# Splitting the norms around the last feed forward into two halves of 128 tokens

## The chip, the cores and the metric

The kernel runs on one core of a Trainium2 chip. The metric is the device time of one launch in microseconds (us), the median of several runs. In the profile PE is TensorE's matmul part and PEld its weight loads, DVE is VectorE, ACT is ScalarE, POOL is GpSimd and SP is SyncE, whose queue issues nearly all transfers.

## The reference

Two transformer blocks stand one behind the other, on 256 tokens of width 1024 in float32. What matters here is the end of the second block, whose last layer takes a neighbourhood attention and then a feed forward on the latent stream alone:

```python
h = gated_residual(h, ml, 1, yl, 1.0)              # yl = attention output @ w_o
h = gated_residual(h, ml, 2, swiglu(ada_in(h, norm_g[i, 2], ml, 2), ffn_w_in[i, 1], ffn_w_out[i, 1]), 0.5)
return rms_norm(h, final_norm_g)

def ada_in(h, g, m, j):
    xn = rms_norm(h, g)                            # over the 1024 features of each token
    return xn * (1.0 + m[:, j, 1][:, None]) + m[:, j, 0][:, None]

def swiglu(x, w_in, w_out):                        # hidden width 2816
    a, b = jnp.split(x @ w_in, 2, axis=-1)
    return (jax.nn.silu(a) * b) @ w_out
```

Both norms that are changed go over the features of a token, so tokens can be taken in any grouping.

## The kernel before

Activations lie feature-major: 8 tiles (KC) of 128 features by 256 tokens (T). `xs[LAT][k]` is the residual of the latent stream. A product adds matmuls into a PSUM tile `acc` (three buffers). Numbers are split in two fp32r parts, so one product step is three matmuls in `mm3` (L400 to L402: whi with hh, wlo with hh, whi with hl), and each matmul has a load of its own 128x128 weights. `load_w` fetches a block of weights (SP queue), and ScalarE (L391) and VectorE (L392) split it into `whi` and `wlo`, four buffers each.

The class `Sq` collects the sum of squares of the residual for the next norm. Its `parts` are slices of the tokens. `add` squares a tile (ScalarE) and adds it up (GpSimd, L484). `end` does the last two tiles of one part, `close` multiplies by a matrix of ones to sum over features (L507 and L508, plain float32, two matmul records each), and `rstd` follows with Ln and Exp on ScalarE (L455, L457).

`grow` makes the 8 output tiles of a product and closes each into the residual (L1053). With an `Sq` the last two tiles, k = 6 and 7, are made part by part: all parts of a PSUM tile share that tile, and as soon as a part of both is there, its norm is closed. `ada` makes the normalized tiles hh and hl from the residual, part by part: two VectorE operations (L1041, L1043) and one of ScalarE (L1042) for each tile. In `ffn` the first pair of products goes through `lead`, which walks over the same parts; all later products take all tokens at once. `ffn` has 22 such pairs (f), then `grow` with the down projection, whose contraction is in three pieces of 8, 7 and 7 tiles; only the last piece carries the `Sq`.

In the earlier feed forwards two streams of 256 tokens are the two parts (`STREAMS`). The attention `nat` of the last layer and the last feed forward have only the latent stream, and before the change one part of 256 tokens. After that the kernel scales the residual by rstd and the final gain into tiles `fin` (L1398 on VectorE for six, L1395 on GpSimd and L1396 on ScalarE for k = 1 and 4) and stores them in three transfers (L1399).

The order on each engine is fixed when the kernel is built: the tile framework orders the instructions of each engine by their readiness in its plan and adds the semaphores, so that an engine's queue may hold work of a later line ahead of work of an earlier one. On the chip each queue runs in that order.

Of the kernel before, what the change touches and what calls it, by code (L numbers as in the profile page):

```python
# [13 lines left out]
ALU = mybir.AluOpType  # L14
# [215 lines left out]
def body(tc, a, off, outs, stop=None):  # L230
# [4 lines left out]
    def tl(pl, shape, tag, dt=F32, bufs=None):  # L235
        uid[0] += 1
        kw = {} if bufs is None else {"bufs": bufs}
        return pl.tile(shape, dt, tag=tag, name=f"{tag}_{uid[0]}", **kw)
# [31 lines left out]
    def V(name, i=None):  # L270
        lo, hi = off["vec"][name]
        return vec[:, lo:hi] if i is None else vec[:, lo + i:lo + i + 1]
# [37 lines left out]
    def G(l, v, j, k):  # L310
        return mod[l][2][:, v, j * 8 + k:j * 8 + k + 1]
# [714 lines left out]
    LAT, CTX = 0, 1  # L1026
    both = (LAT, CTX)
    STREAMS = [slice(0, T), slice(T, 2 * T)]

    def ada(l, j, sq, vs):  # L1030

# [15 lines left out]
    def grow(l, j, vs, prod, sq=None):  # L1047

        N = T * len(vs)

        def close(k, p, i):
            d = xs[vs[i]][k]
            dve.scalar_tensor_tensor(d, p[:, i * T:i * T + T], G(l, vs[i], j, k), d, ALU.mult, ALU.add)  # L1053
            return d

        for k in range(KC - 2 if sq else KC):
            p = acc([P, N])
            prod(k)(p, slice(0, N))
            ds = [close(k, p, i) for i in range(len(vs))]
            if sq:  # L1060
                sq.add(*ds)
        if sq:
            tail = [(k, prod(k), acc([P, N])) for k in (KC - 2, KC - 1)]
            for i, c in enumerate(sq.parts):
                for k, f, p in tail:
                    f(p, c)
                sq.end(i, *[close(k, p, i) for k, f, p in tail])
                sq.close(i)

    def ffn(l, s, j, sq, vs, nparts, every=2):  # L1070

        N = T * len(vs)
        h = ada(l, j, sq, vs)
        nsq = Sq(nparts)
        pace(0)
        with mk(f"ffn{l}{s}") as fp:
            for n, (lo, hi) in enumerate(THIRDS):
                us = []
                if n == 0 and N == T:
                    tl(fp, [P, G2], "gap")  # L1080
                for f in range(lo, hi):
                    if f == 3:
                        pace(every)
                    w = [load_w(a["fin"][2 * l + s, 2 * f + i]) for i in range(2)]
                    if f == 0:
                        pa, pb = lead(w, h, sq.parts)
                    else:
                        pa, pb = acc([P, N]), acc([P, N])
                        mmw(pa, w[0], h)
                        mmw(pb, w[1], h)  # L1090
                    g = tl(fp, [P, N], "sig", bufs=2)
                    sigmoid(g, pa)
                    dve.tensor_tensor(g, pa, g, ALU.mult)
                    dve.tensor_tensor(g, pb, g, ALU.mult)  # L1094
                    u = [tl(fp, [P, N], n_, F32R, bufs=12) for n_ in ("uh", "ul")]
                    split(g, *u)
                    us.append(u)

                def prod(k):
                    w = load_w(a[f"fout{n}"][2 * l + s, k])  # L1100
                    if n == 2 and k == 2:
                        pace(0)
                    return lambda p, c: mmw(p[:, c], w, [cut(u, c) for u in us])
                grow(l, j, vs, prod, nsq if n == 2 else None)
        return nsq
# [157 lines left out]
    def nat(sq):  # L1263
        l, j = 1, 1
        en = ExitStack()
        np_ = en.enter_context(mk("nat"))
        h = ada(l, j, sq, both)
        hl = [cut(t, slice(0, T)) for t in h]
        qs_, ks_, os_ = {}, {}, {}
        vs_ = [tl(np_, [P, D], f"nv{t}") for t in range(4)]  # L1270

        def query(i, p):
            qs_[i] = tl(np_, [P, T], "nq", bufs=3)
            act.activation(qs_[i], p, AF.Copy, scale=0.125)

        def key(i, p):
            ks_[i] = tl(np_, [P, 2 * T], "nk", bufs=3)
            act.activation(ks_[i], p, AF.Copy)

        def project(i):  # L1280
            if i not in qs_:
                query(i, dense(a["nqkv"][i], hl))
            key(i, dense(a["nqkv"][8 + i], h))

        def values(b):
            w = [load_w(a["nv"][b, i]) for i in range(2)]
            for t in range(4):
                p = acc([P, T])
                token_major(w, h, t, p)
                act.activation(vs_[t][:, b * T:b * T + T], p, AF.Copy)  # L1290

        O = {}

        def unit(h2, qt):

            es_ = []
            Ss = [att([P, 2 * T]) for _ in range(2)]
            for hh in range(2):
                rows = slice(64 * hh, 64 * hh + 64)
                pe.matmul(Ss[hh], qs_[h2][rows, qt * P:qt * P + P], ks_[h2][rows, :], start=True, stop=True)  # L1300
            for hh in range(2):
                S = Ss[hh]
                bias = tl(np_, [P, T], "nb", bufs=4)
                nc.sync.dma_start(bias, a["nbias"][2 * h2 + hh, :, qt * T:qt * T + T])
                dve.tensor_tensor(S[:, :T], S[:, :T], bias, ALU.add)
                mx = tl(mini, [P, 1], "mx1")
                dve.tensor_reduce(mx, S, axis=AX.X, op=ALU.max)
                dve.tensor_scalar(mx, mx, -1.0, None, op0=ALU.mult)
                e = tl(np_, [P, 2 * T], "ne", bufs=4)
                sm = tl(mini, [P, 1], "sm1")  # L1310
                act.activation(e, S, AF.Exp, bias=mx, accum_out=sm)
                dve.reciprocal(sm, sm)
                dve.tensor_scalar(e, e, sm, None, op0=ALU.mult)
                es_.append(e)
            yield
            pts = []
            for e in es_:
                tp = nrm([P, 4, P])
                for kt in range(4):
                    pe.transpose(tp[:, kt], e[:, kt * P:kt * P + P], ident)  # L1320
                PT = tl(np_, [P, 4, P], "npt", bufs=4)
                act.activation(PT, tp, AF.Copy)
                pts.append(PT)
            yield
            if qt == 0:
                O[h2] = acc([P, T])
            for kt in range(4):
                for hh in range(2):
                    c = 64 * (2 * h2 + hh)
                    pe.matmul(O[h2][64 * hh:64 * hh + 64, qt * P:qt * P + P], vs_[kt][:, c:c + 64], pts[hh][:, kt],  # L1330
                              start=kt == 0, stop=kt == 3)
            if qt == 1:
                if h2 == 0:
                    tl(np_, [P, G3], "gap")
                os_[h2] = [tl(np_, [P, T], f"{n}{h2}", F32R) for n in ("noh", "nol")]
                split(O[h2], *os_[h2])

        for i, p in enumerate(lead([load_w(a["nqkv"][i]) for i in range(2)], hl, [slice(0, T)])):
            query(i, p)
        project(0)  # L1340
        pace(2)
        for m in range(4):
            put(values, m)
            put(project, 2 * m + 1)
            if m < 3:
                put(project, 2 * m + 2)
                put(lambda: None)
        weave([unit(h2, qt) for h2 in range(8) for qt in range(2)], 1)
        os_ = [os_[i] for i in range(8)]
        nsq = Sq([slice(0, T)])  # L1350

        def prod(k):
            w = load_w(a["nwo"][k])
            return lambda p, c: mmw(p[:, c], w, [cut(o, c) for o in os_])
        grow(l, j, (LAT,), prod, nsq)
        en.close()
        return nsq
# [26 lines left out]
    finish(1, 1)  # L1384
    sq = nat(sq)
    finish(1, 2)
    sq = ffn(1, 1, 2, sq, (LAT,), [slice(0, T)])
    r = sq.rstd(0)
    with mk("fin") as fp:
        for lo, hi in ((0, 3), (3, 6), (6, 8)):  # L1390
            t = tl(fp, [P, hi - lo, T], f"fin{lo}")
            for k in range(lo, hi):
                d = t[:, k - lo]
                if k in (1, 4):
                    pool.tensor_tensor(d, xs[LAT][k], r, ALU.mult)  # L1395
                    act.activation(d, d, AF.Copy, scale=V("fg", k))  # L1396
                else:
                    dve.scalar_tensor_tensor(d, xs[LAT][k], V("fg", k), r, ALU.mult, ALU.mult)  # L1398
            nc.sync.dma_start(outs[0][:, lo:hi], t)  # L1399
    es2.close()  # L1400
    es.close()

# [17 lines left out]
```

## Time and profile before

| what | value |
|---|---|
| median of 3 runs | 2899.43 us (2898.97 to 2900.85) |
| profiled execution | 2906.19 us, span 2904.4 us |
| mean granted TensorE clock | 0.996 |
| busy: PE, PEld, DVE, ACT, POOL | 2867.7, 2551.6, 1973.9, 1409.4, 240.3 us |
| chain that ended last, by engine | PE 91%, DVE 5%, ACT 2%, DMA 1%, issue 1% |

The span goes from the first to the last instruction of the profiled execution; times inside it are us from its start. Matmuls are pipelined and their ends are modelled, so the pace of a row of them is read from the distance of their starts and not from their durations. The granted clock is given as a share of 2.4 GHz; 0.50 is the lower level, 1.2 GHz.

### The profile page before, as it was taken

Reading aid. Unit: us, or ns where it says so; the run is one execution under the profiler, and the core shown is the slowest. Engines: PE = TensorE matmul, PEld = TensorE weight load, DVE = VectorE, ACT = ScalarE, POOL = GpSimd, SP = SyncE. Lnnn points to the kernel's source line nnn. Section 1 sums busy time; section 2 is a strip of 40 time slices with the busy share of each in tenths; the row PEclk is TensorE's granted clock in tenths of the full one; section 3 lists DMA queues with packets and bytes.
Section 4 is the critical chain, followed back from the end, with each engine's and each line's share of the span. In section 5 each row is a group of like instructions: output and inputs, shape, how many; then the busy total and the mean of one; then the engine's idle time right before and its main releaser. Section 6 shows DMA issues by size and latency. Waiting matters only on the chain.

```text
span 2904.4 us, 46127 instructions
## 1 busy us (share of the span) xinstructions
PE 2867.7 (99%) x18084; PEld 2551.6 (88%) x18084; DVE 1973.9 (68%) x3370; ACT 1409.4 (49%) x2487; POOL 240.3 (8%) x216
## 2 busy tenths in 40 slices
PE   8999999999999999999999999999999999999998
PEld 7899999989899988888888888888888888887998
DVE  8787876888887666655776757656566665555665
ACT  7767664677765432334433435332343323444554
POOL 2121100212201000001110101000010000100000
PEclk9999999999999999999999999999999999999999
DMA  6344666544467544443343333444434443333564
GB/s 206 118 125 137 195 202 206 172 132 153 152 211 233 187 149 142 144 148 96 120 142 120 109 116 97 148 146 146 131 116 146 143 146 124 109 93 97 166 183 139
DMA packets 122906, 424.46 MB, mean 146 GB/s; under 512 B 13632, under 2 KB 20160, under 8 KB 122560
## 3 DMA queue, kind: packets, MB, share of 16 engines
q1 hardware_dynamic: 121248, 419.50, 45.9%
q8 instruction: 143, 2.34, 0.3%
q10 hardware_dynamic: 1440, 2.00, 0.2%
q14 instruction: 75, 0.61, 0.1%
HBM read 420.40 MB, written 1.05 MB: 145 GB/s over the span
## 4 chain that ended last, share of the span: by engine, by line
PE 91%; DVE 5%; ACT 2%; DMA 1%; issue 1%; POOL 0%; DVEq 0%; SPq 0%; POOLq 0%; ACTq 0%
PE acc L400 28%; PE acc L402 28%; PE acc L401 28%; DVE wlo L392 1%; PE att L652 1%; ACT whi L391 1%; DMA raw<-in_wmod_dram 1%; PE att L850 1%; PE att L400 1%; PE att L401 1%; PE att L402 1%; PE acc L1330 0%; PE nr L1320 0%; PE att L1300 0%; DVE dump L327 0%
## 5 line engine op out<-in xcount | busy, mean ns | idle before, releaser
L400 PE MATMUL acc<-hh,whi 128*128 128x512 f32 (+2 forms) x3200 | 1052.8, 329 | 12.4 <-ACT hh L528 6.3
L391 ACT ACTIVATE whi<-raw 128x1024 fp32r<-128x1024 f32 (+2 forms) x650 | 678.7, 1045 | 787.9 <-PE acc L402 730.0
L401 PE MATMUL acc<-hh,wlo 128*128 128x512 f32 (+2 forms) x3200 | 1046.1, 327 | 2.8 <-DVE wlo L392 2.8
L402 PE MATMUL acc<-hl,whi 128*128 128x512 f32 (+2 forms) x3200 | 1043.4, 327 | 0.3 <-DVE hl L1043 0.3
L392 DVE TENSOR_TENSOR wlo<-raw,whi 128x1024 fp32r<-128x1024 f32 (+2 forms) x650 | 789.3, 1215 | 331.6 <-ACT whi L391 296.0
L400 PEld LDWEIGHTS acc<-hh,whi 128*128 128x128 f32 x3200 | 605.1, 189 | 74.8 <-ACT hh L528 6.2
L401 PEld LDWEIGHTS acc<-hh,wlo 128*128 128x128 f32 x3200 | 604.1, 189 | 54.8 <-DVE wlo L392 3.5
L402 PEld LDWEIGHTS acc<-hl,whi 128*128 128x128 f32 x3200 | 603.0, 189 | 53.2 <-DVE hl L1043 0.7
L327 DVE SCALAR_TENSOR_TENSOR dump<-raw,cs 128x1024 bf16<-128x1024 f32 x288 | 355.4, 1234 | 260.1 <-DMA raw<-in_wmod_dram 257.4
L400 PE MATMUL acc<-uh,whi 128*128 128x256 f32 (+2 forms) x1258 | 407.0, 324 | 0.0
L402 PE MATMUL acc<-ul,whi 128*128 128x256 f32 (+2 forms) x1258 | 406.2, 323 | 0.2
L401 PE MATMUL acc<-uh,wlo 128*128 128x256 f32 (+2 forms) x1258 | 406.0, 323 | 0.0
L402 PEld LDWEIGHTS acc<-ul,whi 128*128 128x128 f32 x1258 | 237.1, 188 | 19.9 <-DVE ul L450 0.8
L400 PEld LDWEIGHTS acc<-uh,whi 128*128 128x128 f32 x1258 | 236.6, 188 | 19.1
L401 PEld LDWEIGHTS acc<-uh,wlo 128*128 128x128 f32 x1258 | 236.6, 188 | 19.1
L484 POOL TENSOR_TENSOR sqacc<-sqacc,sq 128x256 f32<-128x256 f32 (+2 forms) x60 | 75.6, 1260 | 1854.0 <-ACT sq L479 1756.3
L1053 DVE SCALAR_TENSOR_TENSOR x<-acc,gmod,x 128x256 f32<-128x256 f32 x136 | 65.8, 483 | 154.1 <-PE acc L402 153.5
L461 ACT ACTIVATE sig<-acc 128x512 f32<-128x512 f32 (+1 forms) x88 | 48.0, 546 | 252.2 <-PE acc L402 252.2
L400 PE MATMUL acc<-whi,hh 128*128 128x256 f32 x384 | 109.5, 285 | 0.4 <-ACT pd L1155 0.2
L402 PE MATMUL acc<-wlo,hh 128*128 128x256 f32 x384 | 109.1, 284 | 0.0
L401 PE MATMUL acc<-whi,hl 128*128 128x256 f32 x384 | 108.9, 284 | 0.0
L1094 DVE TENSOR_TENSOR sig<-acc,sig 128x512 f32<-128x512 f32 (+1 forms) x88 | 55.0, 624 | 33.3 <-PE acc L402 27.7
(319 smaller groups left out, 3530.0 us busy)
## 6 DMA issues: line engine op xcount, KB each, us to landing
raw<-in_fin_dram SPq DMA_DIRECT2D x176, 512.0 KB, 3.7
raw<-in_wmod_dram SPq DMA_DIRECT2D x144, 512.0 KB, 4.1
raw<-in_wf_dram SPq DMA_DIRECT2D x128, 512.0 KB, 4.3
raw<-in_win_dram SPq DMA_DIRECT2D x104, 512.0 KB, 3.7
raw<-in_fout_dram SPq DMA_DIRECT2D x64, 448.0 KB, 3.4
raw<-in_fout_dram SPq DMA_DIRECT2D x32, 512.0 KB, 3.6
raw<-in_rin_dram SPq DMA_DIRECT2D x32, 512.0 KB, 3.6
raw<-in_wbr_dram SPq DMA_DIRECT2D x24, 512.0 KB, 3.6
```

The source lines that it names most:

```text
L327: dve.scalar_tensor_tensor(dump, raw, 1.0, cs[:, v], ALU.mult, ALU.mult, accum_out=m[:, v, b:b + 1])
L391: act.activation(hi[:, :n], raw[:, :n], AF.Copy)
L392: dve.tensor_tensor(lo[:, :n], raw[:, :n], hi[:, :n].bitcast(F32), ALU.subtract)
L400: pe.matmul(out, w[0], x[0], start=start, stop=False)
L401: pe.matmul(out, w[1], x[0], start=False, stop=False)
L402: pe.matmul(out, w[0], x[1], start=False, stop=stop)
L461: act.activation(dst, src, AF.Exp, scale=-1.0, **k)
L484: eng.tensor_tensor(self.acc[:, :N], self.acc[:, :N], s[:, :N], ALU.add)
L652: pe.matmul(S[:, c:c + n], q[rows, t0 - q0:t0 - q0 + P], k[rows, 0:n], start=False, stop=i == ns - 1)
L850: pe.matmul(Z[:m, c + lo - k0:c + n], sbk[h2][rows, k0:k0 + m], sbq[h2][rows, lo - q0:Q], start=False, stop=k0 == 0)
L1053: dve.scalar_tensor_tensor(d, p[:, i * T:i * T + T], G(l, vs[i], j, k), d, ALU.mult, ALU.add)
L1094: dve.tensor_tensor(g, pb, g, ALU.mult)
```

## The change

The attention's `Sq` and the last feed forward's `Sq` get two parts of 128 tokens in place of one of 256. Thereby the last two tiles of the attention's output product and of the last down projection, the `ada` of the last feed forward and the first pair of its products are made in two halves. `close` in `grow` takes a slice of tokens in place of a stream's number. The final scaling and the stores go half by half: each half has its own rstd, six VectorE operations, two of GpSimd with two of ScalarE, and three stores whose rows on a partition are two or three pieces of 128 numbers.

```diff
+    HALVES = [slice(0, P), slice(P, T)]
@@ grow
-        def close(k, p, i):
-            d = xs[vs[i]][k]
-            dve.scalar_tensor_tensor(d, p[:, i * T:i * T + T], G(l, vs[i], j, k), d, ALU.mult, ALU.add)
+        def close(k, p, c):
+            v = vs[c.start // T]
+            d = xs[v][k][:, c.start % T:c.start % T + c.stop - c.start]
+            dve.scalar_tensor_tensor(d, p[:, c], G(l, v, j, k), d, ALU.mult, ALU.add)
             return d
...
-            ds = [close(k, p, i) for i in range(len(vs))]
+            ds = [close(k, p, slice(i * T, i * T + T)) for i in range(len(vs))]
...
-                sq.end(i, *[close(k, p, i) for k, f, p in tail])
+                sq.end(i, *[close(k, p, c) for k, f, p in tail])
                 sq.close(i)
@@ nat
-        nsq = Sq([slice(0, T)])
+        nsq = Sq(HALVES)
@@ end of the kernel
-    sq = ffn(1, 1, 2, sq, (LAT,), [slice(0, T)])
-    r = sq.rstd(0)
+    sq = ffn(1, 1, 2, sq, (LAT,), HALVES)
     with mk("fin") as fp:
-        for lo, hi in ((0, 3), (3, 6), (6, 8)):
-            t = tl(fp, [P, hi - lo, T], f"fin{lo}")
...
+        for i, c in enumerate(HALVES):
+            r = sq.rstd(i)
+            for lo, hi in ((0, 3), (3, 6), (6, 8)):
+                t = tl(fp, [P, hi - lo, P], f"fin{i}{lo}")
+                for k in range(lo, hi):
+                    d = t[:, k - lo]
+                    if k in (1, 4):
+                        pool.tensor_tensor(d, xs[LAT][k][:, c], r, ALU.mult)
+                        act.activation(d, d, AF.Copy, scale=V("fg", k))
+                    else:
+                        dve.scalar_tensor_tensor(d, xs[LAT][k][:, c], V("fg", k), r, ALU.mult, ALU.mult)
+                nc.sync.dma_start(outs[0][:, lo:hi, c], t)
```

## Rows read from the trace of the kernel before

**Rows 1.** Busy time and share of each engine, on the page.
```profile
PE 2867.7 (99%) x18084; PEld 2551.6 (88%) x18084; DVE 1973.9 (68%) x3370; ACT 1409.4 (49%) x2487; POOL 240.3 (8%) x216
```

**Rows 2.** First and last matmul of both tail products, in time: start, duration, engine, what.
```profile
2694.57 0.28 PE L400 MATMUL acc<-noh,whi 128*128 128x256 f32 x1
...
2699.90 0.28 PE L402 MATMUL acc<-nol,whi 128*128 128x256 f32 x1
...
2889.15 0.28 PE L400 MATMUL acc<-uh,whi 128*128 128x256 f32 x1
...
2893.98 0.28 PE L402 MATMUL acc<-ul,whi 128*128 128x256 f32 x1
```

**Rows 3.** Stages behind the attention: length, busy PE, PEld, DVE, ACT, POOL, granted clock, DMA.
```profile
2700.00:2704.40 4.40, 1.57 (x6) 0.59 (x4) 2.94 (x6) 2.82 (x6) 0.00 (x0) 0.86 0.49 149
2704.40:2710.00 5.60, 5.60 (x26) 5.60 (x27) 5.42 (x14) 2.98 (x7) 0.00 (x0) 0.50 0.18 72
```

**Rows 4.** Chain that ended last, 2690 to 2720: start, us, what.
```profile
2701.62 0.71 PE nr L508 x2
...
2704.40 0.58 PE acc L400
```

**Rows 5.** The same chain at the kernel's end.
```profile
2894.30 0.50 DVE x L1053
...
2895.29 0.71 PE nr L508 x2
2896.03 0.48 ACT rln L455
...
2896.98 1.05 DVE fin L1398
2898.03 0.87 DVEq L1415
2898.90 1.58 DVE fin L1398 x4
```

**Rows 6.** Weight loads and matmuls of the stick-breaking attention, in order of time.
```profile
685.32 0.19 PEld L870 LDWEIGHTS nr<-t,nonesr 128*128 128x128 f32 x1
685.43 0.19 PEld L869 LDWEIGHTS nr<-t,nonesr 128*128 128x128 f32 x1
685.54 0.19 PEld L870 LDWEIGHTS nr<-t,nonesr 128*128 128x128 f32 x1
...
685.46 0.31 PE L869 MATMUL nr<-t,nonesr 128*128 128x144 f32 x1
...
685.61 0.22 PE L870 MATMUL nr<-t,nonesr 128*128 128x32 f32 x1
```

**Rows 7.** 128-column matmuls in time, and by shape (busy, mean ns).
```profile
2623.14 1.09 PE L1330 MATMUL acc<-npt,nv 128*64 128x128 f32 x16
...
2624.17 1.09 PE L1320 MATMUL nr<-ident,ne 128*128 128x128 f32 x8
...
L1330 PE MATMUL acc<-npt,nv 128*64 128x128 f32 x256 | 18.4, 279 | 0.0
```

**Rows 8.** One operation at two widths, by shape, on VectorE and on ScalarE.
```profile
L906 DVE SCALAR_TENSOR_TENSOR e<-e,rc,e 128x272 f32<-128x272 f32 x8 | 4.0, 495 | 0.0
...
L906 DVE SCALAR_TENSOR_TENSOR e<-e,rc,e 128x144 f32<-128x144 f32 x8 | 2.9, 362 | 0.0
...
L664 ACT ACTIVATE e<-att,mx,qs 128x272 f32<-128x272 f32 x32 | 18.5, 578 | 20.2 <-DVE mx L660 17.6 <-PE att L652 2.1 <-DVE rc L667 0.3
L664 ACT ACTIVATE e<-att,mx,qs 128x144 f32<-128x144 f32 x32 | 14.9, 466 | 0.0
```

**Rows 9.** End of the feed forward with two streams, in order of time.
```profile
2496.41 0.70 PE L508 MATMUL nr<-sqp,ones 128*128 128x256 f32 x2
...
2501.26 0.28 PE L400 MATMUL acc<-hh,whi 128*128 128x256 f32 x1
```

**Rows 10.** Transfers of the result: count, KB each, us to landing.
```profile
out_dram<-fin SPq DMA_DIRECT2D x2, 384.0 KB, 2.7
```

More of the change, by code (lines that the diff above doesn't have):

```diff
@@ L1386, in body @@
     finish(1, 2)
-    sq = ffn(1, 1, 2, sq, (LAT,), [slice(0, T)])
-    r = sq.rstd(0)
+    sq = ffn(1, 1, 2, sq, (LAT,), HALVES)
     with mk("fin") as fp:
-        for lo, hi in ((0, 3), (3, 6), (6, 8)):
-            t = tl(fp, [P, hi - lo, T], f"fin{lo}")
[L1392 to L1399, printed above, removed]
+        for i, c in enumerate(HALVES):
[10 more added lines that the diff above has]
+                nc.sync.dma_start(outs[0][:, lo:hi, c], t)
     es2.close()
```

## The prediction

> **What bounds the kernel now.** I read the page first: TensorE is busy for 99% of the span [rows 1], so a cut pays only where TensorE stands still or runs slowly, and every matmul that is added costs its full price. Then I looked for those places around the two norms that the change touches, in three views. In the order of time, the last two products before each norm (k = 6 and 7) are 48 matmuls that start every 0.1134 us in front of the last feed forward (2694.57 to 2699.90, 47 steps) and 42 that start every 0.1178 us behind it (2889.15 to 2893.98, 41 steps) [rows 2]. In the table by stages, the 4.4 us after the first of these blocks hold six matmuls at a falling clock, and the 5.6 us after that hold 26 matmuls at a granted clock of 0.50, the lower level (1.2 GHz), 0.215 us each [rows 3]. In the chain of waits the path through that hole is norm work: the ones-matmul at 2701.62, then Ln, Exp, the first normalized tile, and TensorE resumes at 2704.40 [rows 4]. At the end of the kernel the same chain is bare: close, square, ones-matmul, Ln, Exp, then 3.50 us of scaling, then the stores, with no matmul beside any of it [rows 5]. So there are two holes: one of 4.39 us (2700.01, one step after the start of the last product, to 2704.40) with a clock loss behind it, and one of 10.3 us (2894.10 to 2904.4).
>
> **What the change adds.** Three blocks of 256-column matmuls become twice as many of 128 columns: the 48 of the attention output product (k = 6, 7), the 48 of the first pair of feed-forward products (`lead` walks over the parts of the norm), and the 42 of the last down projection (k = 6, 7). In `mm3` each matmul loads its own 128x128 weights, so the number of loads doubles too: 276 pairs in place of 138. The whole question is the price of one such pair. Before has no run of 128-column fp32r matmuls, so I bound it.
> The lower end is by columns: half of 0.1134, that is 0.057 us; 128-column matmuls with 64-column weights do start every 0.054 us (1.09 less one duration of 0.28, over 15 steps) [rows 7]. The upper end is by loads. In the stick-breaking attention, fp32r matmuls of 144 and 32 columns alternate, each with its own 128x128 load; their columns need about 0.04 us each on average (88 x 0.1134 / 256), yet the loads start every 0.11 us [rows 6]. Transposes of exactly 128 columns with 128-column weights start every 0.116 us (1.09 less 0.28, over 7 steps), twice as far apart as those with half the weights [rows 7]. So the load sets the pace whenever the columns take less than that, and 256 columns are about the point where both are equal. I take 0.11, the fp32r row, with 0.105 to 0.117 as its own margin, and keep 0.057 for the range.
> 276 x 0.11 = 30.4 us in place of 96 x 0.1134 + 42 x 0.1178 = 15.8: **+14.5**.
> Three of the four closings now have their two ones-matmuls inside the stream of products, where before they stood in a hole: a 256-column ones-matmul is two records, so 4 records x 0.11 = 0.44 each: **+1.3**.
>
> **What it takes away.** In front, the norm of half 0 can run while half 1's products run. Chain: half 0 ends at 2694.57 + 5.3 = 2699.9; close to Exp took 2.88 us at the end of the kernel (2894.10 to 2896.98) [rows 5], about 2.4 with half the columns (below), then one scale and one activation of some 0.4 each: first tile at about 2703.1. Half 1 with its pair of ones-matmuls keeps TensorE until 2705.6. The cover is thus some 2.5 us longer than the chain, and VectorE's two operations per tile at about 0.3 us each (half 0: 16 of them, 4.8 us) stay ahead of TensorE's six matmuls per tile (0.66 us). The same structure exists in the kernel with two streams of 256 tokens, and there the ones-matmul stands among the second stream's products (2496.41) and the next stage's first matmul follows at 2501.26 without a hole [rows 9]. So I take the whole hole as gone, **-4.4**, and the stretch at the lower clock with it: 5.60 us for 26 matmuls against 26 x 0.1134 = 2.95, **-2.65**. What is late next is half 1's norm; it has the 5.3 us of half 0's `lead` matmuls to hide behind. If that cover were gone, up to 2.4 us would come back. The weight buffers of k = 6 and 7 are held some 5.6 us longer than now, but the next weights (f = 1) are not needed before `lead` ends. `lead`'s second accumulator waits for the close of k = 6 of half 1, and that product ends 24 matmuls ahead of `lead`: no wait.
> At the end, half 0's norm, scaling and stores lie beside half 1's products; only half 1's are bare, at 128 columns. What 128 columns are worth: the same scalar_tensor_tensor took 495 ns at 272 and 362 at 144, the same activation 578 and 466 [rows 8], so 0.13 us on VectorE and 0.11 on ScalarE. One close, three activations and a shorter drain of the ones-matmul: 0.13 + 0.34 + 0.05 = 0.5. Six scalings: 0.8 of the 3.50. **-1.3**. GpSimd's and ScalarE's two tiles ride beside them as now. The stores are six in place of three, in pieces of 512 B rather than 2 or 3 KB. Their landing took 2.7 us for 384 KB [rows 10], and I leave the last one at that; half 0's have left the queue by then. If small pieces are slower, up to 1.5 us is added; if the halved traffic helps, 0.3 is saved. Half 0's six scalings (about 2 us) may stand ahead of half 1's close on VectorE: 0 to 0.8 us. The other squares and sums cost the same in two pieces, beside matmuls.
>
> **Sum.** +14.5 + 1.3 - 4.4 - 2.65 - 1.3 = **+7.5 us**. The profiled execution took 2906.2 us with a span of 2904.4, so it lies 6.8 us above the median of the runs, 2899.43; I add the difference to the median: **2906.9 us**. About 0.2% (5.8 us) is what a measurement of this kernel can tell from no change, so this is slower by little more than that.
>
> **A rule beside the rows.** The loads in rows 6 stand 0.11 us apart, and that alone sets my price. The Trainium skill, "TensorE: Matmul & The Clock Gate", section "Back-to-back issue gap", says that a stream of load and matmul pairs at 128 columns settles at about 81 ns each. By that figure the price would be an estimated 276 x 0.081 = 22.4 in place of 30.4, and the sum -0.5 us. Rows 6 and 7 disagree with it for these 4-byte weights.
>
> **Rivals.**
> *Loads overlap better in a long run of pairs (not slower).* Rows 6 show only short runs, between 432-column matmuls. If a long run settles half way between the two bounds, at 0.083, the sum is 276 x (0.083 - 0.11) = -7.5 from mine: **2899.5**, no change. The point of decision is 0.083; below it the change gains. For it: the 0.054 of rows 7. Against it: that row has half the weights, and everything with 128-column weights stands at 0.11 or more. The Trainium skill's figure above would lie just below this case.
> *Columns alone set the price, 0.057.* Then front and end change sides: half 0 ends at 2697.3, its chain at 2699.7, and VectorE's 32 operations of 0.3 us (9.4) and the closes set the end of `lead`, about 2710.5 against 2712.6 now: -2.1. At the end 84 x 0.057 - 4.95 + 0.44 - 1.3 = -1.0. Together **2896.3**.
> *A wait in place of the one removed.* If half 0's ones-matmul stands in TensorE's queue ahead of half 1's products, TensorE waits there as it does now (about 1.2 us, 2894.10 to 2895.29 [rows 5]) at two places, and half 1's norm loses part of its cover: +2.4 to +5: **2909 to 2912**. Against: rows 9.
> *The clock.* The array streams half as many columns per time in these blocks. If that were granted the lower level, as after the hole in rows 3, a pair would cost twice as much; over the front's 192 that is some 20 us: **2927**. Against: the transposes of rows 7 ran at the upper level.
>
> **How the numbers follow.** Load-paced as summed: 0.72, with 2904.5 to 2911 of its own (price 0.105 to 0.117, store, close); of it 0.58 lies above 5.8 us and 0.14 below. Wait: 0.08, slower. Clock: 0.05, slower. Half-way price: 0.08 (0.07 the same, 0.01 faster). Columns: 0.07 (0.03 the same, 0.04 faster, if VectorE is quicker than I take it). So slower 0.71, same 0.24, faster 0.05. The range reaches down to the half-way price and up past the wait: 2899 to 2915.
>
> **What would show it.** In the profile after: 96 + 96 + 84 matmuls of 128 columns in these blocks, starting 0.11 us apart with TensorE's loads back to back; a granted clock of 1.00 between 2700 and 2715; no idle time before `lead`; the last matmul of half 1 some 4.7 us later, relative to the start of k = 6, than now; scaling of half 0 beside matmuls and a bare tail of 9.0 us rather than 10.3. The prediction is wrong if the pairs start less than 0.09 us apart, or if TensorE waits for a ones-matmul between the halves.

## The result and the profile after

| | median of the runs | range | profiled execution | its span | mean granted clock |
|---|---|---|---|---|---|
| before | 2900.14 us (4 runs) | 2898.97 to 2903.92 | 2906.19 us | 2904.4 us | 0.996 |
| changed | 2921.63 us (4 runs) | 2921.29 to 2927.22 | 2921.59 us | 2919.8 us | 0.994 |

The changed kernel is slower: 1.0069 times the kernel before, 95% interval 1.0056 to 1.0082, or 16 to 24 us. Forecast were 2906.9 us and at most 2915. The direction is right; the size is three times too small. Ratios here and below leave out one execution of a later kernel ("end only"), which took 3932 us at a mean granted clock of 0.674.

The page's line of busy times, the answer to [rows 1]: 146 records more, and 20 us more of busy TensorE.

```profile
PE 2888.0 (99%) x18230; PEld 2574.3 (88%) x18230; DVE 1976.2 (68%) x3398; ACT 1411.1 (48%) x2505; POOL 242.5 (8%) x218
```

The first and last matmuls of the two tail products in order of time, against [rows 2], and between them the first one of the next down projection. (Lines of the kernel have moved by up to 3.)

```profile
2691.66 0.22 PE L400 MATMUL acc<-noh,whi 128*128 128x128 f32 x1
...
2703.10 0.28 PE L402 MATMUL acc<-nol,whi 128*128 128x128 f32 x1
...
2766.72 0.28 PE L400 MATMUL acc<-uh,whi 128*128 128x256 f32 x1
...
2901.44 0.22 PE L400 MATMUL acc<-uh,whi 128*128 128x128 f32 x1
...
2911.54 0.28 PE L402 MATMUL acc<-ul,whi 128*128 128x128 f32 x1
```

In the kernel before, the first matmul of that down projection is this one:

```profile
2753.97 0.28 PE L400 MATMUL acc<-uh,whi 128*128 128x256 f32 x1
```

From these rows four stretches can be cut. From the start of k = 6 in front to the first matmul of the next down projection it was 59.40 us and is 75.06: **+15.7**. From there to the start of the last k = 6: -0.5. From there to the end of the span it was 15.25 and is 18.36: **+3.1**. The part ahead of k = 6 came out 2.9 us shorter, in instructions that are the same in both. Sum +15.4, the difference of the spans. In the first stretch another 1.4 us are hidden by a slower pace of the kernel before: behind `lead` its trace takes 41.4 us where that of "end by halves, products whole", with the same instructions, takes 40.0 (last section). So the front costs some 17.

What happens in front, on TensorE in order of time:

```profile
2705.99 0.68 PE L507 MATMUL nr<-sqacc,ones 128*128 128x128 f32 x2 [2.60 <-DVE sqacc L496]
2706.31 0.45 PE L400 MATMUL acc<-hh,whi 128*128 128x128 f32 x1
...
2727.05 0.41 PE L402 MATMUL acc<-hl,whi 128*128 128x128 f32 x1
2727.26 0.52 PE L400 MATMUL acc<-hh,whi 128*128 128x256 f32 x1
```

The hole of 4.39 us is not gone: 2.8 us stand there again (2703.21, one step after the start of the last product, to 2705.99), now ahead of *half 1's* ones-matmul, and the 96 pairs of `lead` behind it take 20.95 us (2706.31 to 2727.26), 0.22 each with two records of that ones-matmul among them. The same stretch by stages (columns as in [rows 3]):

```profile
2697.00:2703.00 6.00, 5.77 (x53) 5.63 (x51) 4.17 (x15) 3.58 (x10) 0.00 (x0) 1.00 0.04 14
2703.00:2706.00 3.00, 0.40 (x5) 0.25 (x4) 2.46 (x7) 2.49 (x4) 0.00 (x0) 1.00 0.00 0
2706.00:2708.00 2.00, 2.00 (x10) 2.00 (x11) 1.32 (x2) 0.31 (x1) 0.00 (x0) 0.54 0.39 141
2708.00:2727.00 19.00, 19.00 (x91) 19.00 (x91) 4.51 (x16) 3.82 (x11) 0.00 (x0) 0.50 0.11 40
2727.00:2730.00 3.00, 3.00 (x16) 3.00 (x16) 1.76 (x2) 2.74 (x5) 0.00 (x0) 0.50 0.00 0
2730.00:2732.00 2.00, 2.00 (x19) 2.00 (x19) 1.45 (x3) 0.44 (x2) 0.00 (x0) 0.99 0.63 164
```

Half 1's products ran at a granted clock of 1.00, 53 records in 6 us. Behind the hole the clock is at 0.50 (1.2 GHz), and it stays there for all of `lead`, although TensorE is busy for 19.00 of 19.00 us. It comes back only after some 3 us of 256-column products. In the kernel before it came back after 5.6 us [rows 3].

Why TensorE stands: half 0's normalized tiles are ready, but half 1's ones-matmul is ahead of their products in TensorE's queue, and it waits for a sum that VectorE makes late. VectorE in order of time:

```profile
2699.18 0.88 DVE L1042 SCALAR_TENSOR_TENSOR xn<-x,amod,rstd 128x128 f32<-128x128 f32 x3 [1.66 <-ACT rstd L457]
...
2703.56 0.35 DVE L1044 SCALAR_TENSOR_TENSOR hl<-xn,mod,hh 128x128 fp32r<-128x128 f32 x1 [0.21 <-ACT hh L1043]
2703.82 0.35 DVE L1055 SCALAR_TENSOR_TENSOR x<-acc,gmod,x 128x128 f32<-128x128 f32 x1
2704.50 1.23 DVE L392 TENSOR_TENSOR wlo<-raw,whi 128x1024 fp32r<-128x1024 f32 x1 [0.33 <-ACT whi L391]
2705.64 0.28 DVE L496 TENSOR_TENSOR sqacc<-sqacc,sqp 128x128 f32<-128x128 f32 x1
```

Half 1's close of k = 6 (L1055) has had its product since about 2700.7: its last matmul starts at 2700.42, 24 pairs ahead of the last of k = 7. It stands behind all 16 `ada` operations of half 0 and starts at 2703.82. Its square on ScalarE (2704.38) follows a weight split of 1.04 us, and its addition (L496) a weight split of 1.23 us on VectorE.

The end of the kernel, in the chain that ended last, against [rows 5]:

```profile
2911.95 0.46 POOL fin L1398
2912.44 0.40 ACT fin L1399
2912.84 0.21 ACT sqp L491
2913.09 0.50 PE nr L508 x2
...
2914.36 0.65 DVE fin L1401
2915.01 0.46 DVEq L1418
2915.47 1.05 DVE fin L1401 x4
```

From the last product (2911.65, one step after its start) to the end there are 8.15 us in place of 10.3. Yet half 0's scaling did not run beside half 1's products: GpSimd's first one starts at 2911.95, though half 0's rstd was there at 2908.26, and it is in the way of half 1's square. The stores, most of them half as large, landed faster than before [rows 10]:

```profile
out_dram<-fin SPq DMA_DIRECT2D x4, 192.0 KB, 2.3
```

### The profile page after: what moved, and what is told of

Its sections match the earlier page's. It is cut to its first block, busy times and chain, and to the rows that moved or that the text cites. A ratio compares the mean times of both kernels' runs of the same rounds, so it can differ in the third digit from the quotient of the medians.

```text
span 2919.8 us, 46473 instructions
## 1 busy us (share of the span) xinstructions
PE 2888.0 (99%) x18230; PEld 2574.3 (88%) x18230; DVE 1976.2 (68%) x3398; ACT 1411.1 (48%) x2505; POOL 242.5 (8%) x218
## 4 chain that ended last, share of the span: by engine, by line
PE 91%; DVE 4%; ACT 2%; issue 1%; DMA 1%; POOL 0%; DVEq 0%; POOLq 0%; ACTq 0%; SPq 0%
PE acc L400 28%; PE acc L402 28%; PE acc L401 28%; DVE wlo L392 1%; ACT whi L391 1%; PE att L652 1%; PE att L400 1%; PE att L401 1%; PE att L402 1%; PE att L850 1%; DMA raw<-in_win_dram 0%; PE acc L1332 0%; PE nr L1322 0%; PE att L1302 0%; DMA raw<-in_wmod_dram 0%
## 5 line engine op out<-in xcount | busy, mean ns | idle before, releaser
L400 PE MATMUL acc<-hh,whi 128*128 128x512 f32 (+3 forms) x3216 | 1060.2, 330 | 7.8 <-ACT hh L528 6.2
L401 PE MATMUL acc<-hh,wlo 128*128 128x512 f32 (+3 forms) x3216 | 1053.5, 328 | 1.9 <-DVE wlo L392 1.9
L402 PE MATMUL acc<-hl,whi 128*128 128x512 f32 (+3 forms) x3216 | 1051.8, 328 | 0.3 <-DVE hl L1044 0.3
L400 PEld LDWEIGHTS acc<-hh,whi 128*128 128x128 f32 x3216 | 611.8, 190 | 69.5 <-ACT hh L528 6.2
L401 PEld LDWEIGHTS acc<-hh,wlo 128*128 128x128 f32 x3216 | 611.7, 190 | 53.4 <-DVE wlo L392 2.4
L402 PEld LDWEIGHTS acc<-hl,whi 128*128 128x128 f32 x3216 | 610.2, 190 | 53.0 <-DVE hl L1044 0.7
L400 PE MATMUL acc<-uh,whi 128*128 128x256 f32 (+3 forms) x1272 | 410.5, 323 | 0.0
L402 PE MATMUL acc<-ul,whi 128*128 128x256 f32 (+3 forms) x1272 | 409.8, 322 | 0.3
L401 PE MATMUL acc<-uh,wlo 128*128 128x256 f32 (+3 forms) x1272 | 409.5, 322 | 0.0
L1055 DVE SCALAR_TENSOR_TENSOR x<-acc,gmod,x 128x256 f32<-128x256 f32 (+1 forms) x140 | 66.7, 476 | 166.0 <-PE acc L402 165.6
```

Source lines behind the costliest of these rows:

```text
L400: pe.matmul(out, w[0], x[0], start=start, stop=False)
L401: pe.matmul(out, w[1], x[0], start=False, stop=False)
L402: pe.matmul(out, w[0], x[1], start=False, stop=stop)
L1055: dve.scalar_tensor_tensor(d, p[:, c], G(l, v, j, k), d, ALU.mult, ALU.add)
```

## The experiments

Two theories. *Hole and clock*: the hole ahead of half 1's ones-matmul costs itself, and behind it the clock falls and stays low while products are narrow. *Loads alone*: the doubled loads cost all of it, at a higher price than forecast. Timed ratios spread by some 0.15% either way, so each experiment is read from its stages too. In the table "front" goes from the start of k = 6 to the first matmul of the next down projection, "end" from the start of the last k = 6 to the end of the span, "low" is the time behind the hole at the lower clock, in whole us; ratios are to the kernel before, run on the same chip.

| kernel | ratio (95%) | front | low | end |
|---|---|---|---|---|
| before | 1 | 59.4 | 7 | 15.3 |
| changed | 1.0069 (1.0056 to 1.0082) | 75.1 | 24 | 18.4 |
| changed again | 1.0076 (1.0064 to 1.0088) | 76.5 | 24 | 18.4 |
| front only | 1.0046 (1.0029 to 1.0063) | 75.1 | 24 | 15.1 |
| end only | 1.0002 (0.9989 to 1.0015) | 55.9 | 0 | 18.4 |
| lead whole | 1.0030 (1.0017 to 1.0044) | 64.1 | 7 | 18.4 |
| half 1's norm behind half 0's lead | 1.0027 (1.0015 to 1.0039) | 64.5 | 0 | 18.4 |
| changed, hole filled | 1.0055 (1.0039 to 1.0072) | 65.6 | 0 | 18.4 |
| the same again | 1.0044 (1.0032 to 1.0056) | 65.6 | 0 | 18.5 |
| before, hole filled | 0.9998 (0.9988 to 1.0007) | 55.9 | 0 | 15.1 |
| end by halves, products whole | 0.9998 (0.9989 to 1.0008) | 58.2 | 7 | 14.4 |
| before, lead in halves | 1.0055 (1.0041 to 1.0069) | 70.6 | 24 | 15.0 |
| hole filled, end by halves | 0.9999 (0.9989 to 1.0008) | 55.9 | 0 | 14.6 |
| own memory for the outputs | 1.0073 (1.0060 to 1.0086) | 75.1 | 24 | 17.9 |

**Front only and end only.** Front only is the changed kernel with the feed forward's norm in one part at the end, and with the scaling and the stores as before:

```diff
-    sq = ffn(1, 1, 2, sq, (LAT,), HALVES)
+    sq = ffn(1, 1, 2, sq, (LAT,), [slice(0, T)])
```

> Only the front of the change is kept: the norm between nwo and the feed forward, the last two nwo products and the first 48 products of the feed forward go by halves; the end is as before. Theory of the hole and the clock: nearly the whole loss sits here, since from the start of nwo's k=6 to the second product of f=1 the changed kernel took 39.6 us against 22.55 before; about +17, so 2916 to 2919 us, with a hole of 2.6 to 2.9 us ahead of half 1's ones-matmuls and the granted clock at 0.50 for some 20 us behind it. Rival, the doubled weight loads alone: 184 of the 276 pairs of 128 columns are here and cost about 9.7 us, and the hole that they fill gives back 4.4: 2904 to 2906 us.

End only has the attention's norm in one part:

```diff
-        nsq = Sq(HALVES)
+        nsq = Sq([slice(0, T)])
```

> Only the end of the change is kept: the last two fout products, the closing norm, the scaling and the stores go by halves; the front is as before. Both theories put it near the forecast of this part: 92 pairs of 128 columns for 46 of 256, +4.8 us, less a bare tail that is 1.3 to 2.3 us shorter: +2.5 to +3.5, so 2902.5 to 2903.7 us. If the two parts with the front's run do not add up to the change's +21.5 us, something else in the kernel has moved too.

(Both miscount: 192 of the 276 pairs are in front, and 84 for 42 at the end, as in the prediction.) The stages answer: the front keeps its 75.1 us alone, and the end its 18.4. The totals, +13 and +1 us with about 4 to 5 us either way, are lower than the stages and add up only within these bounds. End only held a surprise. Its front is that of the kernel before, with the same hole, and the clock did not fall (the stages of its hole and of what followed):

```profile
2697.00:2701.40 4.40, 1.50 (x7) 0.60 (x5) 2.83 (x6) 2.81 (x6) 0.00 (x0) 1.00 0.51 169
2701.40:2707.00 5.60, 5.60 (x46) 5.54 (x47) 5.42 (x14) 2.97 (x7) 0.00 (x0) 1.00 0.14 55
```

The 46 records in 5.6 us stand against 26 in [rows 3]. So the kernel before loses its clock in some executions only: of four traces with this hole and order, in three (its own, "end by halves, products whole" and "before, lead in halves").

**Lead whole.** The changed kernel, but `lead` takes all 256 columns:

```diff
-                        pa, pb = lead(w, h, sq.parts)
+                        pa, pb = lead(w, h, [slice(0, N)] if sq.parts is HALVES else sq.parts)
```

> The changed kernel, but the first 48 products of the feed forward take 256 columns at once and so wait for both halves. Theory of the hole and the clock: the hole before half 1's ones-matmuls stays and one for half 1's tiles comes behind it, so the hole grows to about 4 to 6 us, but the clock comes back some 5 to 6 us after the 256-column products start, as it did in the kernel before; the lead takes about 13.5 us in place of 21, and f=1 starts at the full level: 7 to 9 us under the changed kernel, 2912 to 2915 us. Rival, the loads alone: half of the lead's 96 loads go, which gives about 5 us, and the hole of 4.4 us comes back: 2920 to 2922 us.

Measured 2912.0 us, +8.7 by the ratio, and the front 11 us shorter than changed. Loads alone is out: it gave 2920 to 2922, as much as the changed kernel. Behind the same hole the clock falls and is back 3.4 us after the wide products start:

```profile
2707.30:2710.40 3.10, 1.40 (x4) 1.00 (x4) 2.26 (x6) 1.40 (x5) 0.00 (x0) 0.50 0.57 181
2710.40:2713.80 3.40, 3.36 (x15) 3.36 (x16) 3.36 (x13) 2.45 (x7) 0.00 (x0) 0.50 0.45 143
2713.80:2720.00 6.20, 6.20 (x56) 6.20 (x56) 1.55 (x2) 2.70 (x6) 0.00 (x0) 1.00 0.00 0
```

**Half 1's norm behind half 0's lead.** The changed kernel, but half 1's close is issued after half 0's first four tiles of products:

```diff
-                sq.close(i)
+                if not (sq.defer and i):
+                    sq.close(i)
...
+            mm = some(range(4))
+            with tc.issue_after(mm.ins):
+                sq.close(1)
+            some(range(4, KC))
```

> The changed kernel, but half 1's norm at the front is issued behind the first 24 lead matmuls of half 0, so that TensorE has half 0's products to do while VectorE closes half 1. Theory of the hole and the clock: no stand of over 0.7 us ahead of half 1's ones-matmuls, the granted clock 1.00 through the lead, pairs 0.111 us apart: about 13 us under the changed kernel, 2907 to 2910 us, which is the forecast of the change as it was made. Rival, that the narrow products themselves lower the clock whatever stands before them: the clock at 0.50 in the lead all the same, only the hole gone, 2917 to 2919 us.

Here `some(range(4))` issues half 0's first 24 matmuls of `lead`. TensorE goes from half 1's last product into `lead` without a step lost, and then waits once in it, 0.51 us, for half 1's close of k = 6, whose PSUM tile the second product of `lead` takes over (the prediction had "no wait" there):

```profile
2703.38 0.27 PE L402 MATMUL acc<-nol,whi 128*128 128x128 f32 x1
2703.49 0.28 PE L400 MATMUL acc<-hh,whi 128*128 128x128 f32 x1
...
2704.50 0.33 PE L400 MATMUL acc<-hh,whi 128*128 128x128 f32 x1 [0.51 <-DVE x L1058]
```

The table of stages has the clock at 1.00 through all 96 pairs, 118 records in 13 us:

```profile
2705.00:2718.00 13.00, 13.00 (x118) 13.00 (x118) 8.47 (x22) 7.63 (x17) 0.00 (x0) 1.00 0.26 81
```

The ratio gives +7.8 us (4.4 to 11.3), against +7.5 forecast for the change as it was made. Narrow products alone do not lower the clock.

**Hole filled.** The changed kernel with 24 added matmuls of 256 columns on constant weights behind half 1's last product, into a PSUM tile that nothing reads:

```diff
-                    f(p, c)
+                    mm = f(p, c)
+                if i and sq.spare is not None:
+                    spare(sq.spare, 24, mm)
                 sq.end(i, *[close(k, p, c) for k, f, p in tail])
```

> The changed kernel with 24 matmuls of 256 columns on constant weights added behind half 1's last nwo product, into a PSUM tile that nothing reads: they fill the hole of 2.8 us without shortening it, and every other instruction keeps its place. Theory of the hole and the clock (the narrow products do not lower the clock, the stand before them does): the granted clock stays 1.00 through the lead, its 96 pairs stand 0.111 us apart, and the kernel is 10 to 12 us faster than the changed one, about 8 to 11 us above the kernel before. Rival, that the narrow products lower it by themselves or that the wait alone counts: as the changed kernel, 18 to 21 us above the kernel before.

The wait is not shortened (3.7 us from the start of half 1's last product to the first `lead` matmul, 3.2 to 3.3 in the changed kernel), only its emptiness is taken away. The stages are the filled hole and the `lead` behind it:

```profile
2707.20:2710.00 2.80, 2.80 (x25) 2.80 (x25) 2.25 (x6) 2.50 (x4) 0.00 (x0) 1.00 0.00 0
2710.00:2721.60 11.60, 11.54 (x104) 11.35 (x102) 5.94 (x19) 4.03 (x12) 0.00 (x0) 1.00 0.30 92
```

The clock holds and the front falls by 9.5 us, but four timed runs left the total at +16. So both were timed again, on one chip.

> The changed kernel once more, unaltered, so that it is timed on the same chip as the next kernels. Executions of the kernel before on one chip spread over some 10 us, nearly all of it ahead of nwo's k=6 (its start lay between 2691.6 and 2698.7 us), so totals need many runs. Expected: 18 to 22 us above the kernel before, mean clock 0.993 to 0.995 in every execution, and again some 24 us at the lower level behind the hole.

> The changed kernel with its hole filled by 24 added matmuls, once more, because four timed runs left its total at 16 us above the kernel before while its trace put the stretch from k=6 to the third product 9.5 us below the changed kernel's. If the trace is right and the rest was the spread ahead of that stretch: 9 to 11 us below the changed kernel on the same chip. If the added work costs something that the stretch does not show: 4 to 6 us below.

2925.55 and 2913.00 us: 12.5 us apart, 9.3 by the two ratios. So the first reading's small gain lay within the spread. The mean granted clock parts the two in every execution: 0.993 to 0.995 changed, 0.997 to 0.999 filled (nine and ten runs).

**Before, lead in halves.** Whether width holds the clock down, without any other part of the change: the kernel before, norm in one part, `lead` over two slices.

```diff
-                        pa, pb = lead(w, h, sq.parts)
+                        pa, pb = lead(w, h, [slice(0, P), slice(P, T)] if N == T else sq.parts)
```

> The kernel before, its norm in one part, but the 48 lead products of the last feed forward are taken as 96 of 128 columns. Theory, that behind a hole products of 128 columns leave the clock at the lower level where those of 256 brought it back after 5.6 us: the granted clock at 0.50 through all 96, 0.213 us apart, 20.5 us for the lead in place of 8, and f=1 begins at the lower level too: 12 to 14 us above the kernel before. Rival, that the clock returns after the same 5 to 6 us whatever the width, and only the doubled loads count: 26 pairs at 0.213 and 70 at 0.111, 5 to 6 us above the kernel before.

```profile
2700.00:2704.30 4.30, 1.45 (x6) 0.59 (x4) 2.74 (x5) 2.76 (x6) 0.00 (x0) 1.00 0.51 148
2704.30:2724.80 20.50, 20.35 (x96) 20.22 (x97) 5.49 (x14) 3.32 (x9) 0.00 (x0) 0.52 0.05 21
2724.80:2728.50 3.70, 3.70 (x19) 3.70 (x19) 2.62 (x3) 2.58 (x5) 0.00 (x0) 0.50 0.15 12
```

All 96 pairs at the lower level, 20.5 us, and at least 3.7 us of wide products before it rises: +16 us (12 to 20) by the ratio, against 5 to 6 if the clock had come back as before. By the stages it is 12.4 us (a front of 70.6 against 58.2 with whole products behind the same hole and the same loss of the clock), as the theory had it.

**Before, hole filled.** Five added matmuls stand between the two ones-matmuls of the norm, 18 behind them.

```diff
+            mm = pe.matmul(p, ones, self.acc[:, c], start=True, stop=False)
+            if self.spare is not None:
+                mm = self.spare(5, mm)
+            mm = pe.matmul(p, ones, self.last[i], start=False, stop=True)
+            if self.spare is not None:
+                self.spare(18, mm)
```

> The kernel before with 23 such matmuls added in its own hole at the front: 5 between the two ones-matmuls, 18 behind them. Theory: the hole is as long as it was, but the clock stays at 1.00 and the 26 matmuls that ran at the lower level (0.21 us apart) run at 0.113: 2.4 to 2.8 us faster in the stretch from k=6 to f=1's second product, 0.9991 of the kernel before. Rival, that the lower level after this hole has another cause, or that the added work delays the norm: no gain, or up to 1 us slower.

The front takes 55.9 us with the clock at 1.00, as in the execution of "end only" that kept it by itself, and 2.3 below one that lost it. The total shows nothing, 0.9998: it is a cure for what happens in part of the executions.

**End by halves, products whole.** The front is as before. At the end the last two products take all columns at once (`whole`), and only the norm, the scaling and the stores go by halves.

```diff
-                for k, f, p in tail:
-                    f(p, c)
+                for k, f, p in tail:
+                    if i == 0 or not whole:
+                        f(p, slice(0, N) if whole else c)
```

> Front as in the kernel before; at the end the last two fout products take 256 columns once, and only the closing norm, the scaling and the stores go by halves. If the doubled weight loads are what the end of the change costs, the stretch from the start of fout's k=6 to the end of the span is 4 to 5 us shorter in its products than with products in halves (46 pairs of 256 at 0.113 us in place of 92 at 0.111), while the bare tail is longer than 8.0 us, since both halves' norms then stand behind the last product: 9 to 10 us. Sum 14 to 15 us from k=6 to the end against 15.25 before and 18.36 changed; 0 to 1.5 us faster than the kernel before. If the end's 3.1 us had another cause than the loads, it stays near 18.

(The expectation counts 46 and 92 products again for 42 and 84.) The end takes 14.4 us against 18.4 with products in halves, so the loads are what the end costs. Its bare part is 9.7 us, so the halves there bring 0.6 over before, too little to time.

**Both together.** The kernel before with its hole filled and this end.

> A version made from the findings: the kernel before, its front hole filled with 23 added matmuls, and at the end the last products whole with the norm, the scaling and the stores by halves. By the stages of the two traces 2.3 to 3.7 us come from the front in the executions in which the clock would have fallen, and 0.6 us from the end: 1 to 4 us below the kernel before. Rival: the kernel before keeps its clock in most executions, so that only the 0.6 us of the end is left, within what the runs can tell.

The stages come as expected (55.9 and 14.6), the total does not move: 0.9999. No version here is measurably faster than the kernel before.

**Own memory for the outputs.** The changed kernel with the pool of the `fin` tiles opened ahead of the last feed forward.

> The changed kernel, but the tiles of the scaled outputs have memory of their own in place of memory that the feed forward's tiles give back. If that reuse is what held half 0's scaling until the last product, it now runs beside half 1's products, half 0's stores go out some 4 us earlier, and the bare tail falls from 8.1 to 7.1 to 7.7 us; half 1's Square no longer stands behind a scaling on ScalarE. Rival: half 0's scaling, now ahead of half 1's close on VectorE, delays that close, and the tail stays at 8 us or grows. The total moves by under 1 us either way: this one is read from the trace.

VectorE in order of time:

```profile
2907.82 2.17 DVE L1403 SCALAR_TENSOR_TENSOR fin<-x,vec,rstd 128x128 f32<-128x128 f32 x6 [1.66 <-ACT rstd L457]
2909.92 0.34 DVE L1055 SCALAR_TENSOR_TENSOR x<-acc,gmod,x 128x128 f32<-128x128 f32 x1
...
2911.39 0.35 DVE L1055 SCALAR_TENSOR_TENSOR x<-acc,gmod,x 128x128 f32<-128x128 f32 x1 [0.47 <-PE acc L402]
```

Now the scaling follows its rstd, and half 1's last close waits only for TensorE. The bare tail is 7.66 us in place of 8.15. The reuse of memory was the hold.

## Why the prediction was wrong

**The price of a pair was right.** The 96 pairs in front, with half 0's ones-matmuls among them, took 11.5 us up to one step after the last (10.6 and 0.4 forecast), and in the trace they start 0.111 us apart. The rivals of a half-way price and of columns alone fall with that. The Trainium skill, "TensorE: Matmul & The Clock Gate", section "Back-to-back issue gap", would have had 81 ns; here the measurement decides against it for these weights.

**The step that failed first: "I take the whole hole as gone", -4.4.** The chain of half 0 was as forecast (rstd at 2699.15, first tiles a us later, well before half 1's end). What the step leaned on next was that half 1's norm "has the 5.3 us of half 0's `lead` matmuls to hide behind". It cannot, since in TensorE's queue its ones-matmul stands *ahead* of them. It also came late, behind half 0's 16 VectorE operations and two weight splits. From half 1's last product to the first `lead` matmul it is 3.1 us, of which 0.4 was counted: +2.7. I had a wait as a rival, but looked for it at half 0's ones-matmul. The comparison with the two-stream case [rows 9] did not carry over, though there too a part's products take about 5 us. What differs is the order in the queues. On VectorE the second stream's close of k = 6 (L1053) stands behind three `ada` operations of the first stream and not behind 16, and on TensorE three products of the first stream stand ahead of the second stream's ones-matmul (2501.76), which waits for almost nothing:

```profile
2498.11 1.28 DVE L1041 SCALAR_TENSOR_TENSOR xn<-x,amod,rstd 128x256 f32<-128x256 f32 x3 [2.20 <-ACT rstd L457]
2499.31 0.48 DVE L1053 SCALAR_TENSOR_TENSOR xc<-acc,gmod,xc 128x256 f32<-128x256 f32 x1
...
2501.50 0.28 PE L402 MATMUL acc<-hl,whi 128*128 128x256 f32 x1
2501.76 0.70 PE L507 MATMUL nr<-sqacc,ones 128*128 128x256 f32 x2
```

**The step that failed most: the lower clock gone, -2.65.** A shorter hole lowered it all the same, and the narrow products kept it low. `lead` took 20.95 us against 10.56 forecast, +10.4, and the first products of f = 1 some +1.2 more. Against that, the wait behind `lead` that before shows (1.66 us in the profile, 1.8 from start to start less one step) is gone in this run, -1.8. The forecast of the front was 4.1 (192 x 0.11 - 96 x 0.1134, + 0.9, - 4.4, - 2.65). With 0.5 for the pairs it comes to 4.1 + 0.5 + 2.7 + 10.4 + 1.2 - 1.8 = 17.1, as measured. "Half 1's norm behind half 0's lead" changes only the order, and gives the forecast's total; "hole filled" keeps the wait and gives back the clock alone. Of the 13 us missed, the clock is then about 10 net, and the hole and the pairs are the rest. The rival "the clock" had the right price per pair at the lower level, but the wrong cause: it had the narrow products lower it, and they ran at 1.00 wherever no hole stood before them.
The Trainium skill, the same page, section "HAM oscillation — how this bites in real kernels", tells of a kernel whose waits sent TensorE back to the half rate again and again, so that each following block began slow. The 0.50 behind the holes agrees with it.

**The end was right in sum, partly by luck.** Forecast +3.4, measured +3.1: its pairs and ones-matmuls were 0.5 dearer, and the bare tail was 8.15 in place of 9.0, though half 0's scaling was held back. In that tail the chain up to the first scaling took 2.7 us (2.4 forecast), the six scalings 2.16 (2.7 forecast), and from the last of them to the end there were 3.3 (3.9 before, which the forecast left as it was):

```profile
2914.36 2.16 DVE L1401 SCALAR_TENSOR_TENSOR fin<-x,vec,rstd 128x128 f32<-128x128 f32 x6 [0.29 <-ACT rstd L457]
```

## What to carry to other kernels

Splitting a norm to hide its chain only works if the second part's norm is not queued ahead of the first part's products: look at the order on the matmul engine and on the engine that closes, not only at the data's dependences. Here a matmul that brings its own weights cost nearly the same at 128 columns as at 256 (0.111 and 0.113 us), so each split product doubles its price. And a stand of a few us on TensorE is priced by what runs behind it: wide products had the clock back after 3.4 to 5.6 us, narrow ones carried the lower level for as long as they lasted, some 21 us.

## What the runs showed of the hardware

At the lower level a pair of 128 columns took 0.213 us, the same as a matmul of 256 columns there [rows 3] and twice its own 0.111. Its weight loads start 0.213 us apart there as well, so the pace of the loads falls with the clock too.

Whether the clock falls behind the same hole can differ between executions: of four traces of the 4.4 us hole (two stands, of 0.7 and 2.1 us, around the second ones-matmul) it fell in three, of five of the 2.8 us hole (both of the changed kernel, front only, lead whole and own memory) in all. The mean granted clock agrees for all 15 timed executions of front only, changed again and own memory: 0.993 to 0.995, where the kernel before had 0.995 to 0.999. Why the narrow products do not win the clock back stays open.

Executions of one kernel spread over 10 us and more, and the traces show where much of that comes from: the clock as well. Ahead of the first k = 6, where all kernels here are the same, the 14 traces hold none to three stretches of 3.4 us at the lower level, most of them near 260 or 2510 us, other ones in other executions; what brings them about was not taken apart. At half the clock each costs an estimated 1.7 us. In the two traces without any, k = 6 starts at 2689.9 and 2690.7; in the four with three, at 2694.9 to 2697.4. One such place, in "changed again" and then in "the same again" (the filled kernel's second run), which had none:

```profile
245.00:252.00 7.00, 7.00 (x36) 6.25 (x36) 4.35 (x15) 3.83 (x15) 1.66 (x2) 0.76 0.44 145
245.00:252.00 7.00, 6.57 (x52) 6.00 (x50) 5.48 (x17) 5.00 (x16) 1.99 (x3) 1.00 0.28 76
```

At a granted clock of 1.00 the 256-column matmuls have two paces, 0.1133 and 0.1178 us; [rows 2] hold both. Behind the first k = 6 the slower one comes in stretches of some 60 us or twice that, placed differently in each execution. From the first matmul of the next down projection to the last k = 6 it is 132.5 to 133.0 us in the traces without a whole such stretch, 134.6 to 135.2 with one and 136.8 with a double one. In "before, hole filled" a stretch of 194 us (820 to 1014), which no other trace has, cost some 7 us and put its k = 6 at 2698.5, the latest of all. The granted clock in the profile does not tell the two paces apart, and what sets the pace stays open.
